# Up projection of an MLP by seven products a pair: the order of the products, a weight difference kept in a tile of its own, and the point from which results are stored

## The chip, the core and the metric

The kernel runs on one core of a Trainium2 chip. The metric is the device time of one execution in microseconds (us); the median of the runs shown is compared. A difference of 0.2% is about 3.1 us here.

## The reference, cut to what matters

The whole layer is computed: a projection, an mLSTM and a forgetting attention side by side, cross attention into 256 memory tokens, then the MLP and a last norm. The change touches the first matrix product of the MLP.

```
u = relu(rmsnorm(x) @ w_ff1)     # x: 1024 tokens x 1024, w_ff1: 1024 x 4096
x = x + (u * u) @ w_ff2          # w_ff2: 4096 x 1024
return rmsnorm(x, ln_f)
```

All of it is float32.

## The kernel before, in words

**Three passes for a product.** TensorE multiplies a rounded type, `fp32r`. A float32 operand is split in a high part (ScalarE, L132) and the rest (VectorE, L133); `mm3` (L182) then makes three matmuls, low times high, high times low and high times high, with lines L184, L185 and L186.

**Seven products for a pair.** The up projection takes the 32 output tiles of 128 in 16 pairs. Of a pair, weights and activations are cut in 2 x 2 blocks (two output tiles, two halves of the 1024 inputs, two halves of the 1024 tokens), and the four result blocks come out of seven block products with sums of blocks, numbered 1 to 7, in place of eight. The right sides (`H`: blocks 11, 21, t1, t2, 22, t3, t4) are made once and lie in SBUF in seven `act` tiles. The left sides are made for each pair by `left_up` (L1185) in three groups: group 0 loads two raw tiles and splits the halves for products 1 and 2 and the half for product 4 (`r_b`, `r_c`), then GpSimd turns the raw tiles into sums and differences in place; group 1 gives products 5 and 6, group 2 gives 7 and 3. One block product is 4 x 3 = 12 matmuls of 128 x 512.

**Three banks for a pair.** Product 1 goes to PSUM bank a, 5 to bank c, 6 to bank b. Product 2 is added into a, 3 into c, 7 and then 4 into b. Between two products of one bank the first has to be read: after 1 ScalarE copies the bank to `p1` (L1339); after 5, 6, 3, 7 and 4 VectorE adds it to a result block (`add`, L1326). So TensorE cannot start 2, 3, 7 or 4 before that read is done. Each finished block is squared after a relu on ScalarE (L1315, L1316).

**The order.** `jobs` lists the products in order. For pairs 2 to 13 it is 1, 4 of the pair before, 5, 2, 6, 3, 7 (L1216); the first two pairs are interleaved product by product, and so are the last two (L1217). `prepare` (L1227) calls a group's left side five jobs ahead. At each job one function of `later` is called: `put_right` (L1369) gives a pair seven such functions after its product 4, which make the right sides of the down projection from the four blocks and store them to DRAM (`put`, L1362: split, then two stores; the high part goes through `r_d` and `r_e` in turn, two tiles each). At every eighth job `stretch` (L1422) loads a 128 x 1024 piece of the residual (`x2d`, L1427), and four jobs later VectorE multiplies it by a row (L1430) and it is stored.

**Who sets the rest.** A scheduler of the framework places each instruction on its engine's queue when the program is built. The engines then run their queues strictly in order, and every DMA is issued by SyncE (SP) in order too. The tiles are shared through pools: three `wh` and three `wl` tiles for a left side's two parts, two tiles each for `r_b`, `r_c`, `r_p`, `r_d`, `r_e`, five `w4`, and eight PSUM banks.

**After it.** The down projection (L1505) loads the stored right sides in the `act` tiles that the up projection frees (`rights`, L1463), and x2d as well (`x2_load`, L1484).

Of the kernel before, what the change touches and what calls it, by code (L numbers as in the profile page):

```python
# [44 lines left out]
def hybrid_layer(ctx: ExitStack, tc: tile.TileContext, a: dict, out: bass.AP):  # L45
# [1139 lines left out]
    def left_up(p_, group):  # L1185
# [5 lines left out]
        hi, lo = (sb(t, [P, 1024], 3, F32R) for t in ("wh", "wl"))  # L1191
        split(hi, lo, (r1, r2, r1)[group])
        if group == 0:
            h22, l22 = (w2(t, dt=F32R) for t in ("bc" if p_ else "ay"))
            split(h22, l22, x22)
            cuts[p_, 4] = both((h22, l22), lambda t: t.rearrange("p (k c) -> p k c", k=4))

            by = g if p_ > 1 else v
            by.tensor_tensor(out=x21, in0=x21, in1=x22, op=ALU.add)
            sub(x22, x21, x11, by)  # L1200
            sub(x12, x12, x22, by)
            sub(x11, h22.bitcast(F32), x22, by)
            by.tensor_tensor(out=x11, in0=x11, in1=l22.bitcast(F32), op=ALU.add)
        for e in range(2):
            cuts[p_, ((1, 2), (5, 6), (7, 3))[group][e]] = both((hi, lo), lambda t: t[:, e * TH : e * TH + TH].rearrange("p (k c) -> p k c", k=4))
        if group == 2:
            del raws[p_]

    raws = {}
    RIGHTS = {1: "11", 2: "21", 5: "t1", 6: "t2", 3: "22", 7: "t3", 4: "t4"}  # L1210
    NP = len(todo)
    both_of = lambda p_: [(q_, i) for i in RIGHTS for q_ in (p_, p_ + 1)]
    jobs = both_of(0)
    for p_ in range(2, NP - 2):

        jobs += [(p_, 1)] + ([(p_ - 1, 4)] if p_ > 2 else []) + [(p_, i) for i in (5, 2, 6, 3, 7)]  # L1216
    jobs += [(NP - 2, 1), (NP - 3, 4)] + both_of(NP - 2)[1:]  # L1217
    GROUP = {1: 0, 2: 0, 5: 1, 6: 1, 7: 2, 3: 2}
# [94 lines left out]
    def squared(x, y):  # L1313

        s.activation(x, y, AF.Relu)  # L1315
        s.activation(x, x, AF.Square)  # L1316

    class Pair:


        def __init__(self, p_):
            self.p_ = p_
            self.u = {}

# [3 lines left out]
        def run(self, i, l):  # L1328
# [8 lines left out]
            if i == 1:  # L1337
                self.p1 = w2("p") if 1 < self.p_ < NP - 2 else row[:, TH * (self.p_ % 2) :][:, :TH]
                s.activation(self.p1, ps, AF.Copy)  # L1339
# [3 lines left out]
            elif i == 5:  # L1343
                t = w4()
                u["22"], self.t1 = t[:, :TH], t[:, TH:]
                self.add(u["22"], ps, self.p1)
# [15 lines left out]
    def put(dst, x):  # L1362

        hi = rotate("d", "e").bitcast(F32R)
        split(hi, x.bitcast(F32R), x)
        load(dst[0], hi.bitcast(F32))
        load(dst[1], x)

    def put_right(b, k, pair):  # L1369

        u11, u12, u21, u22 = (pair.u[c] for c in ("11", "12", "21", "22"))
        t1 = pair.t1
        to = lambda c: [right[b][ORDER.index(c), :, p_, k] for p_ in range(2)]
        t = {}

# [11 lines left out]
        def four():  # L1387
            sub(t[4], t[2], u21)
            put(to("22"), u22)

        return [one, two, lambda: put(to("t3"), u12), four, lambda: put(to("21"), u21), lambda: put(to("t2"), t[2]), lambda: put(to("t4"), t[4])]

# [42 lines left out]
    for at, (p_, i) in enumerate(jobs):  # L1435
# [6 lines left out]
        if at == 30:  # L1442
            to_row(row, inv, 8, rowd[3:4], bank)
        if at > 30 and at % 4 == 0 and stretches:
            stretch(stretches[0])
            if at % 8 == 4:
                stretches.pop(0)
        if at == len(jobs) - 3:
            lefts = left(a["w_ff2q"][0, 0])
        if later:  # L1450
            later.pop(0)()
        pair = pairs.setdefault(p_, Pair(p_))
        pair.run(i, cuts.pop((p_, i)))
        if i == 4:
            b, k = todo[p_][:2]
            later += put_right(b, k, pair) if b < NB - 1 else put_plain(k, pair)
            del pairs[p_]
# [186 lines left out]
```

## Time and profile before

| | us |
|---|---|
| median of 3 runs (1546.37 to 1550.0) | 1548.31 |
| the profiled execution's own time | 1549.03 |
| its span, first to last instruction | 1547.3 |
| TensorE (PE) busy | 1510.3 |
| VectorE (DVE) busy | 1100.9 |
| ScalarE (ACT) busy | 718.8 |
| GpSimd (POOL) busy | 483.4 |

The up projection runs from about 886 to 1216 us of the span. In the profile PE is the matmul engine. A row of the timeline gives the start, the time it took, the engine, the line, what is written and read, and in square brackets how long the engine had been idle before it and what ended that. In a row of a group, the number after the bar is the busy time, then the mean in ns, then the idle time before these instructions and its releasers. A matmul's end is modelled, and matmuls overlap, so the distance from start to start is what one costs.

### The profile page before, as it was taken

The page shows a single profiled execution, that of the slowest core. Times are in us where ns is not written, and L with a number is a line of the kernel's source. Part 1 is how long each engine was busy: PE and PEld are TensorE (multiplying, and loading weights), DVE is VectorE, ACT ScalarE, POOL GpSimd, SP SyncE. Part 2 cuts the span into 40 slices and gives each one's busy share as a digit, 9 for nine tenths or more (in the row PEclk, how much of TensorE's full clock was granted, in tenths as well). Part 3 has the DMA queues.
Part 4 walks back from the last instruction along what each step waited for, and adds up shares of the span by engine and source line. Part 5 has one row for each costly group of instructions (what it writes and reads, how often), then busy time and mean ns, then how long its engine had stood idle before and what let it go on. Part 6 is the DMA issues. An engine that isn't in the chain of part 4 may idle for free.

```text
span 1547.3 us, 21934 instructions
## 1 busy us (share of the span) xinstructions
PE 1510.3 (98%) x7729; PEld 1261.5 (82%) x7729; DVE 1100.9 (71%) x1722; ACT 718.8 (46%) x1337; POOL 483.4 (31%) x515
## 2 busy tenths in 40 slices
PE   8999999999999999999999999999999999999997
PEld 8878888889898887788888788777778778888887
DVE  7656676665788874854457987777777787777766
ACT  7324343334678763543344456555455532222234
POOL 0002130413455441511110034453444644433310
PEclk9999999999999999999999999999999999999998
DMA  6422223436887948953344446776776965556623
GB/s 220 122 79 82 100 100 114 130 130 162 253 248 219 305 166 286 327 176 124 122 147 153 150 148 230 268 253 230 250 243 219 370 251 217 219 207 227 236 92 110
DMA packets 118075, 297.25 MB, mean 192 GB/s; under 512 B 13118, under 2 KB 27768, under 8 KB 111820
## 3 DMA queue, kind: packets, MB, share of 16 engines
q1 hardware_dynamic: 117964, 295.84, 55.9%
q8 instruction: 61, 1.00, 0.3%
q14 instruction: 50, 0.41, 0.1%
HBM read 199.08 MB, written 96.71 MB: 191 GB/s over the span
## 4 chain that ended last, share of the span: by engine, by line
PE 82%; DMA 7%; DVE 6%; issue 2%; ACT 2%; POOL 0%; SPq 0%; DVEq 0%; POOLq 0%; ACTq 0%
PE tp L184 7%; PE tp L186 7%; PE tp L185 7%; PE mm L184 5%; PE sc L184 5%; PE sc L186 5%; PE sc L185 5%; PE mm L186 5%; PE mm L185 5%; PE m L184 5%; PE m L186 5%; PE m L185 5%; PE ov L184 2%; PE ov L185 2%; PE ov L186 2%
## 5 line engine op out<-in xcount | busy, mean ns | idle before, releaser
L184 PE MATMUL tp<-act,wl 128*128 128x512 f32 (+1 forms) x448 | 176.1, 394 | 4.8 <-DVE r_f L1326 3.4
L185 PE MATMUL tp<-act,wh 128*128 128x512 f32 (+1 forms) x448 | 175.3, 391 | 0.0
L186 PE MATMUL tp<-act,wh 128*128 128x512 f32 (+1 forms) x448 | 174.9, 392 | 0.0
L133 DVE TENSOR_TENSOR wl<-wr,wh 128x1024 fp32r<-128x1024 f32 (+2 forms) x99 | 126.3, 1276 | 26.7 <-ACT wh L132 26.3
L132 ACT ACTIVATE wh<-wr 128x1024 fp32r<-128x1024 f32 (+2 forms) x99 | 99.0, 1000 | 94.5 <-PE tp L186 32.7
L184 PE MATMUL mm<-act,wl 128*128 128x512 f32 (+1 forms) x336 | 130.6, 389 | 3.5 <-DVE r_e L1071 1.3
L186 PE MATMUL mm<-act,wh 128*128 128x512 f32 (+1 forms) x336 | 129.0, 384 | 0.0
L185 PE MATMUL mm<-act,wh 128*128 128x512 f32 (+1 forms) x336 | 128.8, 383 | 0.0
L184 PE MATMUL m<-act,wl 128*128 128x512 f32 (+1 forms) x312 | 120.3, 386 | 0.9 <-DVE r_a L916 0.9
L186 PE MATMUL m<-act,wh 128*128 128x512 f32 (+1 forms) x312 | 119.3, 382 | 0.0
L185 PE MATMUL m<-act,wh 128*128 128x512 f32 (+1 forms) x312 | 119.1, 382 | 0.0
L184 PEld LDWEIGHTS tp<-act,wl 128*128 128x128 f32 x448 | 84.2, 188 | 25.4 <-DVE r_f L1326 3.8
L184 PE MATMUL sc<-act,wl 128*128 128x512 f32 (+1 forms) x252 | 98.7, 392 | 3.8 <-DVE r_f L1326 2.3
L1410 POOL TENSOR_TENSOR z<-wr 128x256 f32<-128x256 f32 x56 | 53.5, 976 | 150.4 <-DMA wr<-w_ff2q 127.9
L186 PEld LDWEIGHTS tp<-act,wh 128*128 128x128 f32 x448 | 84.2, 188 | 19.2
L185 PEld LDWEIGHTS tp<-act,wh 128*128 128x128 f32 x448 | 84.2, 188 | 18.8
L185 PE MATMUL sc<-act,wh 128*128 128x512 f32 (+1 forms) x252 | 98.4, 390 | 0.0
L186 PE MATMUL sc<-act,wh 128*128 128x512 f32 (+1 forms) x252 | 98.3, 391 | 0.0
L132 ACT ACTIVATE w<-wr 128x768 fp32r<-128x768 f32 (+2 forms) x31 | 25.5, 824 | 127.3 <-PE tp L186 70.3
L132 ACT ACTIVATE wh<-z 128x1024 fp32r<-128x1024 f32 (+1 forms) x54 | 55.5, 1027 | 61.1 <-POOL z L1410 27.3
L133 DVE TENSOR_TENSOR wl<-z,wh 128x1024 fp32r<-128x1024 f32 (+1 forms) x54 | 73.1, 1353 | 12.4 <-ACT wh L132 12.3
L184 PEld LDWEIGHTS mm<-act,wl 128*128 128x128 f32 x336 | 63.3, 188 | 17.2 <-DVE wl L133 2.1
(676 smaller groups left out, 4236.8 us busy)
## 6 DMA issues: line engine op xcount, KB each, us to landing
act<-right SPq DMA_DIRECT2D x35, 1024.0 KB
right<-w SPq DMA_DIRECT2D x56, 256.0 KB
wr<-w_ff2q SPq DMA_DIRECT2D x28, 512.0 KB
act<-fqk SPq DMA_DIRECT2D x48, 256.0 KB
wr<-w_in SPq DMA_DIRECT2D x20, 512.0 KB
wr<-w_ff SPq DMA_DIRECT2D x20, 512.0 KB
right<-r_e SPq DMA_DIRECT2D x35, 256.0 KB
right<-r_d SPq DMA_DIRECT2D x35, 256.0 KB
```

The source lines that it names most:

```text
L132: s.activation(hi, src, AF.Copy)
L133: return v.tensor_tensor(out=lo, in0=src, in1=hi.bitcast(F32), op=ALU.subtract)
L184: nc.tensor.matmul(ps, w[1], x[0], start=first, stop=False, skip_group_check=more)
L185: nc.tensor.matmul(ps, w[0], x[1], start=False, stop=False, skip_group_check=more)
L186: nc.tensor.matmul(ps, w[0], x[0], start=False, stop=last, skip_group_check=more)
L1410: g.tensor_tensor(out=o, in0=x, in1=y, op=op)
```

## The change

- **Order of the products.** For pairs 2 to 14 it is now 1, 5, 6, 2, 4 of the pair before, 3, 7. The last pair has an order of its own: 1, 6, 4 of pair 14, 5, 7, 2, 3, 4. The first two pairs keep theirs. Of two products into one bank (1 and 2, 5 and 3, 6 and 7, 7 and 4) at least two others stand between from pair 2 on; before, one stood between 6 and 7 and one between 7 and 4.
- **A tile for a difference.** The difference x11 - x21, which product 7 needs, was computed back from the split parts of x22 into the raw tile by two GpSimd instructions at the end of a group's chain. It is now the first instruction of the chain and goes to an `r_e` tile (`thirds`). The chain has four instructions and not five; group 2 splits its two halves apart (two instructions of 512 columns and not one of 1024, on ScalarE and on VectorE). `put` now uses `r_d` alone.
- **Stores.** `put_right` is called twice: four functions after product 7 and three after product 4. Of `later`, two are called at a job when more than five wait.
- **x2d pieces.** `stretch` loads at jobs divisible by 8 and multiplies seven jobs later, and not four.
- The tiles of the last pairs change: `p1` takes `r_p` there too, and the last pair's block 22 takes the half of a `w4` tile that pair 14 doesn't use.

```diff
@@ -1189,32 +1189,36 @@
         r1, r2 = raws[p_]
         x11, x12, x21, x22 = r1[:, :TH], r1[:, TH:], r2[:, :TH], r2[:, TH:]
         hi, lo = (sb(t, [P, 1024], 3, F32R) for t in ("wh", "wl"))
-        split(hi, lo, (r1, r2, r1)[group])
+        if group < 2:
+            split(hi, lo, (r1, r2)[group])
+        else:
+            for c, x in ((slice(0, TH), x12), (slice(TH, 2 * TH), thirds.pop(p_))):
+                split(hi[:, c], lo[:, c], x)
         if group == 0:
             h22, l22 = (w2(t, dt=F32R) for t in ("bc" if p_ else "ay"))
             split(h22, l22, x22)
             cuts[p_, 4] = both((h22, l22), lambda t: t.rearrange("p (k c) -> p k c", k=4))
 
             by = g if p_ > 1 else v
+            s3 = thirds[p_] = w2("e") if p_ > 1 else x11
+            sub(s3, x11, x21, by)
             by.tensor_tensor(out=x21, in0=x21, in1=x22, op=ALU.add)
-            sub(x22, x21, x11, by)
+            sub(x22, x22, s3, by)
             sub(x12, x12, x22, by)
-            sub(x11, h22.bitcast(F32), x22, by)
-            by.tensor_tensor(out=x11, in0=x11, in1=l22.bitcast(F32), op=ALU.add)
         for e in range(2):
-            cuts[p_, ((1, 2), (5, 6), (7, 3))[group][e]] = both((hi, lo), lambda t: t[:, e * TH : e * TH + TH].rearrange("p (k c) -> p k c", k=4))
+            cuts[p_, ((1, 2), (5, 6), (3, 7))[group][e]] = both((hi, lo), lambda t: t[:, e * TH : e * TH + TH].rearrange("p (k c) -> p k c", k=4))
         if group == 2:
             del raws[p_]
 
-    raws = {}
+    raws, thirds = {}, {}
     RIGHTS = {1: "11", 2: "21", 5: "t1", 6: "t2", 3: "22", 7: "t3", 4: "t4"}
     NP = len(todo)
     both_of = lambda p_: [(q_, i) for i in RIGHTS for q_ in (p_, p_ + 1)]
     jobs = both_of(0)
-    for p_ in range(2, NP - 2):
-
-        jobs += [(p_, 1)] + ([(p_ - 1, 4)] if p_ > 2 else []) + [(p_, i) for i in (5, 2, 6, 3, 7)]
-    jobs += [(NP - 2, 1), (NP - 3, 4)] + both_of(NP - 2)[1:]
+    for p_ in range(2, NP - 1):
+
+        jobs += [(p_, i) for i in (1, 5, 6, 2)] + ([(p_ - 1, 4)] if p_ > 2 else []) + [(p_, 3), (p_, 7)]
+    jobs += [(NP - 1, 1), (NP - 1, 6), (NP - 2, 4)] + [(NP - 1, i) for i in (5, 7, 2, 3, 4)]
     GROUP = {1: 0, 2: 0, 5: 1, 6: 1, 7: 2, 3: 2}
     first = {}
     for at, (p_, i) in enumerate(jobs):
...
@@ -1361,17 +1372,16 @@
 
     def put(dst, x):
 
-        hi = rotate("d", "e").bitcast(F32R)
+        hi = w2("d", dt=F32R)
         split(hi, x.bitcast(F32R), x)
         load(dst[0], hi.bitcast(F32))
         load(dst[1], x)
 
-    def put_right(b, k, pair):
-
-        u11, u12, u21, u22 = (pair.u[c] for c in ("11", "12", "21", "22"))
-        t1 = pair.t1
+    def put_right(b, k, pair, last):
+
+        u, t1, t = pair.u, pair.t1, pair.t
+        u11, u12, u22 = (u[c] for c in ("11", "12", "22"))
         to = lambda c: [right[b][ORDER.index(c), :, p_, k] for p_ in range(2)]
-        t = {}
 
         def one():
             sub(t1, u12, u11)
@@ -1385,10 +1395,12 @@
             load(to("t1")[1], t1)
 
         def four():
-            sub(t[4], t[2], u21)
-            put(to("22"), u22)
-
-        return [one, two, lambda: put(to("t3"), u12), four, lambda: put(to("21"), u21), lambda: put(to("t2"), t[2]), lambda: put(to("t4"), t[4])]
+            sub(t[4], t[2], u["21"])
+            put(to("21"), u["21"])
+
+        if last:
+            return [four, lambda: put(to("t2"), t[2]), lambda: put(to("t4"), t[4])]
+        return [one, two, lambda: put(to("t3"), u12), lambda: put(to("22"), u22)]
 
     def put_plain(k, pair):
         f = lambda i, hf: lambda: put([plain[2 * i + k, :, p_, hf] for p_ in range(2)], pair.u[f"{i + 1}{hf + 1}"])
@@ -1441,19 +1453,23 @@
             norm_factors(1)
         if at == 30:
             to_row(row, inv, 8, rowd[3:4], bank)
-        if at > 30 and at % 4 == 0 and stretches:
+        if at > 31 and at % 8 in (0, 7) and stretches:
             stretch(stretches[0])
-            if at % 8 == 4:
+            if at % 8 == 7:
                 stretches.pop(0)
         if at == len(jobs) - 3:
             lefts = left(a["w_ff2q"][0, 0])
-        if later:
-            later.pop(0)()
+        for _ in range(2 if len(later) > 5 else 1):
+            if later:
+                later.pop(0)()
         pair = pairs.setdefault(p_, Pair(p_))
         pair.run(i, cuts.pop((p_, i)))
+        b, k = todo[p_][:2]
+        if i in (7, 4) and b < NB - 1:
+            later += put_right(b, k, pair, i == 4)
+        elif i == 4:
+            later += put_plain(k, pair)
         if i == 4:
-            b, k = todo[p_][:2]
-            later += put_right(b, k, pair) if b < NB - 1 else put_plain(k, pair)
             del pairs[p_]
     for f in later:
         f()
```

Left out of the diff are the new tiles of the last pairs (the last bullet). The rows below are each engine's queue as the program has it, in order: line, operation, tile written, tiles read, partitions by columns. The numbers in a name tell one tile from another.

VectorE before, around the addition of product 4 of a pair, after the x2d piece's multiplication (L1430): `sc_1884` holds product 4 and `sc_1908` product 6 of the next pair, `r_b_1898` and `r_c_1899` are the two parts of the half that the left side of the pair after that needs for its own product 4, and `wl_1897` is its group 0.

```order
L1430 TENSOR_TENSOR w4_1923_10699<-w4_1923_10699,row_79 128x1024
L1326 TENSOR_TENSOR r_p_1868_10331<-sc_1884_10421,r_p_1868_10331 128x512
L133 TENSOR_TENSOR r_c_1899_10527<-wr_1895_10519,r_b_1898_10526 128x512
L1166 TENSOR_TENSOR w4_1916_10663<-w4_1916_10663,r_p_1868_10331 128x512
L133 TENSOR_TENSOR r_p_1868_10331<-r_p_1868_10331,r_e_1931_10746 128x512
L133 TENSOR_TENSOR w4_1916_10663<-w4_1916_10663,r_d_1934_10766 128x512
L1326 TENSOR_TENSOR r_f_1909_10598<-sc_1908_10585,r_p_1891_10495 128x512
L133 TENSOR_TENSOR wl_1897_10523<-wr_1894_10518,wh_1896_10522 128x1024
L133 TENSOR_TENSOR w4_1916_10663<-w4_1916_10663,r_e_1935_10788 128x512
L1326 TENSOR_TENSOR r_f_1909_10598<-tp_1901_10540,r_f_1909_10598 128x512
```

The addition of product 6 to `r_f_1909` stands seventh, behind the piece, the addition of 4, the `r_c` split, a difference and two splits of `put`. The same place after the change, where `r_p_1855` gets product 4 from `sc_1866`, `r_f_1892` gets product 6 from `sc_1891` and then 3 from `tp_1881`, and `wl_1886` and `wl_1894` are groups 0 and 1 of one left side:

```order
L1332 TENSOR_TENSOR r_f_1892_10428<-sc_1891_10415,r_p_1880_10375 128x512
L133 TENSOR_TENSOR wl_1886_10399<-z4_1883_10394,wh_1885_10398 128x1024
L1442 TENSOR_TENSOR w4_1905_10543<-w4_1905_10543,row_79 128x1024
L1332 TENSOR_TENSOR r_p_1855_10207<-sc_1866_10247,r_p_1855_10207 128x512
L133 TENSOR_TENSOR r_c_1888_10403<-z4_1884_10395,r_b_1887_10402 128x512
L1166 TENSOR_TENSOR w4_1890_10411<-w4_1890_10411,r_p_1855_10207 128x512
L1332 TENSOR_TENSOR r_f_1892_10428<-tp_1881_10379,r_f_1892_10428 128x512
L133 TENSOR_TENSOR r_p_1855_10207<-r_p_1855_10207,r_d_1898_10475 128x512
L133 TENSOR_TENSOR w4_1890_10411<-w4_1890_10411,r_d_1899_10495 128x512
L133 TENSOR_TENSOR wl_1894_10431<-z4_1884_10395,wh_1893_10430 128x1024
```

The addition of 6 now stands first, ahead of the piece, and the addition of 4 behind it. Behind 4 stand the same splits and the addition of 3, and group 1's `wl` ends the list.

GpSimd before, the chain of a left side (`wr_1894` and `wr_1895` are the raw tiles; a row writes one half of a tile), with the sum x21 + x22 of the next left side ahead of it and a difference of a finished pair's blocks behind it:

```order
L1199 TENSOR_TENSOR z4_1918_10683<-z4_1918_10683 128x512
L1166 TENSOR_TENSOR wr_1895_10519<-wr_1895_10519,wr_1894_10518 128x512
L1166 TENSOR_TENSOR wr_1894_10518<-wr_1894_10518,wr_1895_10519 128x512
L1166 TENSOR_TENSOR wr_1894_10518<-r_b_1898_10526,wr_1895_10519 128x512
L1203 TENSOR_TENSOR wr_1894_10518<-wr_1894_10518,r_c_1899_10527 128x512
L1166 TENSOR_TENSOR r_f_1909_10598<-w4_1902_10553,r_f_1909_10598 128x512
```

And after, where `z4_1883` and `z4_1884` are the raw tiles of such a chain, the first two rows and `wr_1908` and `wr_1909` being of the next left side:

```order
L1166 TENSOR_TENSOR r_e_1914_10574<-wr_1908_10562,wr_1909_10563 128x512
L1205 TENSOR_TENSOR wr_1909_10563<-wr_1909_10563 128x512
L1166 TENSOR_TENSOR z4_1884_10395<-z4_1884_10395,r_e_1889_10406 128x512
L1166 TENSOR_TENSOR z4_1883_10394<-z4_1883_10394,z4_1884_10395 128x512
L1166 TENSOR_TENSOR r_f_1892_10428<-w4_1882_10392,r_f_1892_10428 128x512
```

The instructions that read `r_b` and `r_c` are gone, and one that writes an `r_e` tile stands first.

SyncE before, from a piece's load (L1427) to its store (L1431):

```order
L1427 DMA w4_1923_10699<-x2d_7240 128x1024
L1366 DMA right3_7244<-r_d_1927_10722 128x512
L1366 DMA right3_7244<-r_e_1924_10701 128x512
L1367 DMA right3_7244<-w4_1878_10387 128x512
L1367 DMA right3_7244<-r_f_1885_10434 128x512
L1366 DMA right3_7244<-r_d_1934_10766 128x512
L1431 DMA x2d_7240<-w4_1923_10699 128x1024
```

And after:

```order
L1439 DMA w4_1905_10543<-x2d_7240 128x1024
L1378 DMA right3_7244<-r_f_1867_10260 128x512
L1377 DMA right3_7244<-r_d_1897_10454 128x512
L1378 DMA right3_7244<-w4_1857_10224 128x512
L1443 DMA x2d_7240<-w4_1905_10543 128x1024
```

Between load and store stand three stores of `put` and not five, though three more jobs lie between them.

More of the change, by code (lines that the diff above doesn't have):

```diff
@@ L1316, in squared @@
         s.activation(x, x, AF.Square)
+    unused = []
     class Pair:
@@ L1322, in __init__ @@
             self.p_ = p_
-            self.u = {}
+            self.u, self.t = {}, {}
         def add(self, out_, ps, x):
@@ L1337, in run @@
             if i == 1:
-                self.p1 = w2("p") if 1 < self.p_ < NP - 2 else row[:, TH * (self.p_ % 2) :][:, :TH]
+                self.p1 = w2("p") if self.p_ > 1 else row[:, TH * (self.p_ % 2) :][:, :TH]
                 s.activation(self.p1, ps, AF.Copy)
@@ L1343, in run @@
             elif i == 5:
-                t = w4()
-                u["22"], self.t1 = t[:, :TH], t[:, TH:]
+                if self.p_ == NP - 1:
+                    u["22"] = unused.pop()
+                else:
+                    t = w4()
+                    u["22"], self.t1 = t[:, :TH], t[:, TH:]
+                    if self.p_ == NP - 2:
+                        unused.append(self.t1)
                 self.add(u["22"], ps, self.p1)
```

## Prediction, on record before the run

> **What bounds the kernel now.** I began with the page's line of busy times:
>
> ```profile
> PE 1510.3 (98%) x7729; PEld 1261.5 (82%) x7729; DVE 1100.9 (71%) x1722; ACT 718.8 (46%) x1337; POOL 483.4 (31%) x515
> ```
>
> TensorE is busy for 98%, so a change that removes none of its matmuls can gain only where it waits. Next I read the windows of the up projection and of the passage to the down projection. The columns are the stretch, its length, the busy time of PE, PEld, DVE, ACT and POOL, the granted clock, the DMA share and GB/s:
>
> ```profile
> 906.00:1206.00 300.00, 289.70 (x1231) 231.42 (x1230) 229.67 (x254) 169.15 (x261) 143.65 (x93) 0.99 0.69 238
> 1206.00:1260.00 54.00, 53.60 (x229) 42.51 (x228) 45.41 (x59) 23.11 (x31) 30.22 (x30) 1.00 1.00 379
> ```
>
> PE idles 10.3 us of 300 in the first stretch and 0.4 of 54 in the second, where the DMA engines are full. 16 pairs of 7 products of 12 matmuls are 1344 matmuls, as many after as before. The timeline of PE has the waits of the stage one by one (start, time, what ran, and the idle before it):
>
> ```profile
> 889.51 0.50 PE L184 MATMUL tp<-act,wl 128*128 128x512 f32 x1 [0.74 <-ACT row L1339]
> 1000.65 0.50 PE L184 MATMUL tp<-act,wl 128*128 128x512 f32 x1 [3.37 <-DVE r_f L1326]
> 1021.50 0.50 PE L184 MATMUL mm<-act,wl 128*128 128x512 f32 x1 [0.99 <-DVE wl L133]
> 1063.30 0.50 PE L184 MATMUL sc<-act,wl 128*128 128x512 f32 x1 [2.34 <-DVE r_f L1326]
> 1063.64 0.52 PE L185 MATMUL sc<-act,wh 128*128 128x512 f32 x1
> ...
> 1067.29 0.39 PE L185 MATMUL sc<-act,wh 128*128 128x512 f32 x1
> 1067.51 0.39 PE L186 MATMUL sc<-act,wh 128*128 128x512 f32 x1
> ...
> 1126.25 0.50 PE L184 MATMUL ov<-act,wl 128*128 128x512 f32 x1 [2.18 <-DVE r_f L1326]
> 1147.52 0.50 PE L184 MATMUL sc<-act,wl 128*128 128x512 f32 x1 [1.42 <-DVE wl L133]
> 1210.07 0.50 PE L184 MATMUL tp<-act,r_c 128*128 128x512 f32 x1 [0.19 <-DVE w L1326]
> 1239.49 0.50 PE L184 MATMUL mm<-act,wl 128*128 128x512 f32 x1 [0.21 <-DVE wl L133]
> ```
>
> Three large waits end on `r_f` of L1326: product 7 waits for the addition of 6 out of the bank that 7 needs. Two end on `wl`, a left side's low part. A matmul is some 0.39 us long but the next starts 0.22 to 0.235 us after it (1067.29 to 1067.51), so a product of 12 lasts 2.8 us and a pair 19.6, and an idle of x costs x + 0.16. To see why VectorE was late I took its own timeline ahead of the wait at 1063.30, and the issue of the piece's load:
>
> ```profile
> 1051.46 0.42 SPq L1427 DMA_DIRECT2D w<-x2d  x1
> ```
>
> ```profile
> 1056.90 1.23 DVE L1430 TENSOR_TENSOR w<-w,row 128x1024 f32<-128x1024 f32 x1 [2.22 <-DMA w<-x2d]
> 1058.04 0.68 DVE L1326 TENSOR_TENSOR r_p<-sc,r_p 128x512 f32<-128x512 f32 x1
> 1058.64 0.69 DVE L133 TENSOR_TENSOR r_c<-wr,r_b 128x512 fp32r<-128x512 f32 x1
> 1060.09 1.16 DVE L1166 TENSOR_TENSOR w<-w,r_p 128x512 f32<-128x512 f32 x1 [0.76 <-ACT r_p L1316]
> 1061.35 0.69 DVE L133 TENSOR_TENSOR r_p<-r_p,r_e 128x512 fp32r<-128x512 f32 x1
> 1061.96 0.69 DVE L133 TENSOR_TENSOR w<-w,r_d 128x512 fp32r<-128x512 f32 x1
> 1062.56 0.68 DVE L1326 TENSOR_TENSOR r_f<-sc,r_p 128x512 f32<-128x512 f32 x1
> 1063.16 1.22 DVE L133 TENSOR_TENSOR wl<-wr,wh 128x1024 fp32r<-128x1024 f32 x1
> ```
>
> The piece landed 5.4 us after its issue, VectorE stood 2.22 us for it, and six instructions later the addition of 6 ended at 1063.24, just before PE went on. The group of that line sums it up:
>
> ```profile
> L1430 DVE TENSOR_TENSOR w<-w,row 128x1024 f32<-128x1024 f32 x8 | 10.2, 1275 | 19.0 <-DMA w<-x2d 19.0
> ```
>
> All eight pieces were waited for, 2.4 us on the average. Only one product (2.8 us) lies between 6 and 7, so what VectorE loses there reaches PE.
>
> **The waits that go.** After the change 3 or more products stand between 6 and 7 as the pairs run (2, 4, 3), that is 8.4 us and not 2.8, and the addition of 6 stands ahead of the piece in VectorE's queue. The longest wait, 3.37 us, is less than the 5.6 us gained, so I count the three waits for `r_f` gone: 3.37 + 2.34 + 2.18 = 7.89. The two on `wl` (0.99 + 1.42 = 2.41) come from the same delay: `wl` is the instruction behind the addition of 6 in the list above. SyncE's queue also moves: the piece's load is issued behind a store of `put` that follows product 1 of the pair, some 1.8 us after that product (two ACT steps of about 0.64, as the splits below, and the issue's 0.42); the multiplication cannot come before group 0's `wl`, which waits for the end of product 2, 8.4 us behind product 1. That gives the load 9 us for its 5.4, so the 19.0 us of VectorE go too. What is late next is group 1's `wl`, below.
>
> Five waits: 10.30 idle, and 5 x 0.16 = 0.8 for the pipeline. The first step after a wait is 0.34 and not 0.235 (1063.30 to 1063.64): 5 x 0.1 = 0.5. And from 1063.64 to 1067.29 PE took 3.65 us for ten steps that are 2.34 else: 1.3 at half clock, following the wait. Sum 12.9. The Trainium skill ("TensorE: Matmul & The Clock Gate", What's actually happening) has the clock fall after an idle window of about 3.4 us that runs free of the program. This trace shows the fall behind an idle of 2.34 and none behind 3.37, so it doesn't bear out a threshold on the wait alone; if the 1.3 us hung on something else than this wait, they would stay, and the forecast below would be 1.3 us higher.
>
> The waits of 0.74 (first pairs, order kept) and 0.19 and 0.21 (last pairs) I leave as they are; if the last two went too, 0.4 + 2 x 0.16 = 0.7 more would be gained.
>
> **The new chain.** Product 4 of a pair now stands fifth in the next pair, and frees `r_b` and `r_c`, two tiles each. Call its end E. From there: ACT splits `r_b`, DVE `r_c`, GpSimd subtracts in the raw tile, ACT makes group 1's `wh`, DVE its `wl`, and product 5 of the pair after needs it at E + 8.4 (3, 7 and 1 lie between). Before, seven products did, 19.6 us. The rows at such an end, and the groups of the steps in 906 to 1206:
>
> ```profile
> 1011.72 0.39 PE L186 MATMUL ov<-act,wh 128*128 128x512 f32 x1
> ```
>
> ```profile
> 1011.92 0.64 ACT L132 ACTIVATE r_b<-wr 128x512 fp32r<-128x512 f32 x1 [1.84 <-PE tp L186]
> 1011.92 0.69 DVE L1326 TENSOR_TENSOR r_p<-tp,r_p 128x512 f32<-128x512 f32 x1 [1.11 <-PE tp L186]
> ```
>
> ```profile
> L133 DVE TENSOR_TENSOR wl<-wr,wh 128x1024 fp32r<-128x1024 f32 x22 | 33.2, 1513 | 5.1 <-ACT wh L132 5.1
> L1166 DVE TENSOR_TENSOR w<-w,r_p 128x512 f32<-128x512 f32 x12 | 15.1, 1260 | 2.6 <-ACT r_p L1316 2.5
> L133 DVE TENSOR_TENSOR r_c<-z,r_b 128x512 fp32r<-128x512 f32 x7 | 7.0, 998 | 0.3 <-ACT r_b L132 0.3
> L133 DVE TENSOR_TENSOR w<-w,r_d 128x512 fp32r<-128x512 f32 x21 | 17.5, 835 | 1.6 <-ACT r_d L132 1.1
> L133 DVE TENSOR_TENSOR r_p<-r_p,r_e 128x512 fp32r<-128x512 f32 x6 | 6.3, 1049 | 0.1
> ```
>
> ```profile
> L132 ACT ACTIVATE wh<-wr 128x1024 fp32r<-128x1024 f32 x22 | 23.2, 1053 | 10.1 <-POOL wr L1203 5.1 <-POOL wr L1166 2.3 <-PE sc L186 1.7
> L1315 ACT ACTIVATE r_p<-r_p 128x512 f32<-128x512 f32 x12 | 7.6, 630 | 11.3 <-DVE r_p L1326 11.1
> ```
>
> ```profile
> L1166 POOL TENSOR_TENSOR z<-z,z 128x512 f32<-128x512 f32 x14 | 21.1, 1505 | 30.2 <-DVE wl L133 17.7 <-DVE r_c L133 11.8 <-POOL z L1199 0.7
> L1166 POOL TENSOR_TENSOR z<-r_b,z 128x512 f32<-128x512 f32 x7 | 14.0, 1994 | 0.0
> L1203 POOL TENSOR_TENSOR z<-z,r_c 128x512 f32<-128x512 f32 x7 | 11.9, 1702 | 0.5
> ```
>
> VectorE's queue behind E holds, with the means, the addition of 4 (0.2 after E, 0.7), `r_c` (0.85, between 0.69 and 1.0), the wait for the relu and the square (2 x 0.63 behind the addition), the difference (1.26), the addition of 3 (0.7), two low parts of `put` (0.85 and 1.05) and `wl` (1.5): it ends at E + 7.5, 0.9 us early. In the eight pairs with a piece, group 0's `wl` starts at E - 1.75 (the end of product 2 and an ACT split of 1.05 behind it), ends at E - 0.2, and the piece's 1.28 puts the addition of 4 at E + 1.25 and `wl`'s end, the same row of steps on, at E + 8.5 to 8.8. That is 0.1 to 0.4 us late; I take 0.25, the middle, in eight pairs: **+2.0**. The bounds are 0 (at the quickest rows of the timeline, 0.69 and 1.22, it is on time) and 0.4 + 0.16 in each of the 12 pairs, 6.7.
>
> **What costs nothing.** GpSimd loses the 1.99 and the 1.70 us of two instructions per pair and gains one of 1.5. Group 2's two splits of 512 are 2 x 0.63 on ACT for 1.05, and 2 x 0.69 on DVE for 1.22: 0.2 more on each. They are hidden by engines that are idle for 131 us (ACT) and 70 us (DVE) of the 300; without cover they would cost 0.2 in each of 13 pairs, 2.6, which the chain's upper bound holds.
>
> **The passage to the down projection.** There the DMA engines are full (1.00, 379 GB/s), and the last pair's own order frees the `act` tiles later; a tile of 128 x 2048 float32 is 1 MB, 2.8 us at that rate. If one comes late, PE waits for up to that; if `r_d`'s stores block the queue as well, 4. Before, PE lost 0.4 in 54 us there. Bounds 0 and 4; I take **+0.5**, nearest to what the window shows.
>
> **The sum.** 1549.03 - 12.9 + 2.0 + 0.5 = 1538.6 for an execution like the profiled one, which lies 0.7 above the median of the runs: 1537.9.
>
> **The rivals.** *Half of the gain is given back:* the chain late in all 12 pairs by 0.4 + 0.16, 6.7 and not 2.0: 1537.9 + 4.7 = 1542.6 (the passage at its bound gives 1541.4). For it: the waits of ACT's `wh` for GpSimd (5.1 and 2.3 above) show that this hand-off is already the slow one. Against it: two GpSimd steps are gone from it. *The waits only move:* VectorE's additions are late for another reason than the piece, and others take their place: about 1548. Against it: all three waits for `r_f` lie behind a wait for a piece.
>
> *Slower:* `put` uses two `r_d` tiles and not four tiles, so ACT's split waits for the store of two puts ago; the VectorE split of `put` waits with it, and behind it in the queue stands group 1's `wl`, for which PE waits in every pair. It decides from the point where `wl` ends later than E + 8.4; at E + 9.6 it is 1.24 + 0.16 = 1.4 in 12 pairs, 17 us: 1549.03 - 12.9 + 17 + 0.5 - 0.7 = 1553. It makes up for the whole gain from 1.1 us a pair. For it: the piece's load took 5.4 us to land, and two puts are 5.6 us apart at one a job. Against it: VectorE waited only 1.1 us in 21 splits for `r_d`. The Trainium skill ("GPSIMD Engine Reference", Key points) says that GpSimd shares its SBUF interfaces with VectorE and contends with its instructions of two SBUF inputs; the trace agrees, with `wl` at 1.22 alone and 1.51 in the mean. It would lengthen this chain, and the means used here hold it already.
>
> **How the numbers follow.** 0.2%, 3.1 us, is about what a measurement of this kernel can tell from no change. The forecast has 0.70 (its own range 1534 to 1541), half the gain given back 0.14, no change 0.08, slower 0.08. Faster is the first two: 0.84. The range begins at 1533.5: no late chain, no cost in the passage and the 0.7 of the last pairs gone give 1537.9 - 3.2 = 1534.7, and runs scatter by 1 to 2 us. It ends at 1545.5, where the chain costs 6.7 and the passage 3.4, and leaves out the last two cases.
>
> **What the profile after would show.** Right: no wait for a piece on DVE's L1442, no wait of PE for `r_f`, PE's idle in the stage at about 3 us and not 11.4 (10.30 + 0.74 + 0.19 + 0.21), small waits for group 1's `wl` in pairs with a piece. Wrong: waits of PE for `wl` in most pairs, 0.4 us or more each; ACT waiting for stores ahead of `r_d`; PE waiting for `act` loads behind the last pair; or the same waits for additions at other products.

## The result and the profile after

The changed kernel takes 1535.09 us (median of 4 runs, 1534.38 to 1535.7), the kernel before 1547.58 beside it. The ratio is 0.9911, with a 95% interval of 0.9899 to 0.9924: faster by 12.5 us. The forecast was 1537.9 us, faster, in a range of 1533.5 to 1545.5.

The page's line of busy times, and the windows of the up projection and of the passage behind it:

```profile
PE 1507.4 (98%) x7729; PEld 1263.2 (82%) x7729; DVE 1104.6 (72%) x1736; ACT 721.8 (47%) x1353; POOL 456.4 (30%) x501
```

```profile
906.00:1206.00 300.00, 300.00 (x1288) 241.89 (x1287) 241.96 (x282) 183.25 (x293) 127.21 (x89) 1.00 0.71 254
1206.00:1260.00 54.00, 54.00 (x234) 43.53 (x233) 45.06 (x60) 16.16 (x19) 24.64 (x24) 1.00 0.82 310
```

PE has no idle left in either stretch, where it had 10.3 and 0.4 us, and its clock is 1.00 and not 0.99. The whole list of PE's waits from 886 to 1262 us is one row, the wait in the first pairs, which the change leaves alone (what waited, for whom, us in total, times, longest):

```profile
PE tp L184 <- ACT row L1345: 0.7, 1, 0.7
```

It stands 0.44 us earlier than before, and that is all that the work ahead of the stage adds:

```profile
889.07 0.50 PE L184 MATMUL tp<-act,wl 128*128 128x512 f32 x1 [0.73 <-ACT row L1345]
```

The spans are 1547.3 and 1532.6, 14.7 apart. So 14.2 us come from the stage and the passage: the 10.7 of idle, a restart of about 0.26 behind each of the seven waits, and the half clock behind one. The profiled execution of before is 1.45 us above the median of its runs and that of after 0.7 below, which is why their difference is larger than the 12.5.

### The profile page after: what moved, and what is told of

It is laid out like the page before. It is cut to its first block, busy times and chain, and to the rows that moved or that the text cites. A ratio compares the mean times of both kernels' runs of the same rounds, so it can differ in the third digit from the quotient of the medians.

```text
span 1532.6 us, 21930 instructions
## 1 busy us (share of the span) xinstructions
PE 1507.4 (98%) x7729; PEld 1263.2 (82%) x7729; DVE 1104.6 (72%) x1736; ACT 721.8 (47%) x1353; POOL 456.4 (30%) x501
## 4 chain that ended last, share of the span: by engine, by line
PE 92%; DMA 3%; DVE 2%; ACT 1%; issue 1%; POOL 0%; SPq 0%; DVEq 0%; POOLq 0%; ACTq 0%
PE tp L184 8%; PE tp L186 8%; PE tp L185 8%; PE sc L184 6%; PE sc L186 6%; PE sc L185 6%; PE mm L184 6%; PE mm L186 6%; PE mm L185 6%; PE m L184 6%; PE m L186 6%; PE m L185 6%; PE ov L779 2%; PE ov L184 2%; PE ov L185 2%; PE ov L186 2%
## 5 line engine op out<-in xcount | busy, mean ns | idle before, releaser
L184 PE MATMUL tp<-act,wl 128*128 128x512 f32 (+1 forms) x440 | 172.5, 393 | 0.7 <-ACT row L1345 0.7
L185 PE MATMUL tp<-act,wh 128*128 128x512 f32 (+1 forms) x440 | 172.2, 391 | 0.0
L186 PE MATMUL tp<-act,wh 128*128 128x512 f32 (+1 forms) x440 | 172.0, 392 | 0.0
L132 ACT ACTIVATE wh<-wr 128x1024 fp32r<-128x1024 f32 (+3 forms) x100 | 96.1, 962 | 104.0 <-PE tp L186 39.7
L133 DVE TENSOR_TENSOR wl<-wr,wh 128x1024 fp32r<-128x1024 f32 (+3 forms) x100 | 120.2, 1203 | 21.7 <-ACT wh L132 21.3
L186 PE MATMUL mm<-act,wh 128*128 128x512 f32 (+1 forms) x344 | 132.2, 384 | 0.0
L185 PE MATMUL mm<-act,wh 128*128 128x512 f32 (+1 forms) x344 | 132.0, 384 | 0.0
L132 ACT ACTIVATE wh<-z 128x1024 fp32r<-128x1024 f32 (+2 forms) x55 | 52.5, 956 | 66.0 <-POOL z L1422 29.4
L133 DVE TENSOR_TENSOR wl<-z,wh 128x1024 fp32r<-128x1024 f32 (+2 forms) x55 | 67.0, 1219 | 12.0 <-ACT wh L132 11.9
```

Source lines behind the costliest of these rows:

```text
L132: s.activation(hi, src, AF.Copy)
L133: return v.tensor_tensor(out=lo, in0=src, in1=hi.bitcast(F32), op=ALU.subtract)
L184: nc.tensor.matmul(ps, w[1], x[0], start=first, stop=False, skip_group_check=more)
L185: nc.tensor.matmul(ps, w[0], x[1], start=False, stop=False, skip_group_check=more)
L186: nc.tensor.matmul(ps, w[0], x[0], start=False, stop=last, skip_group_check=more)
```

## The experiments

All are compared with the kernel before on the same chip, whose median lay between 1547 and 1551 us from chip to chip, so the ratios are what compares. "The two GpSimd instructions" are the last two of the old chain of a left side, which compute x11 - x21 from `r_b` and `r_c` for product 7.

| kernel | order | pieces | the two GpSimd instructions | ratio to before (95%) | PE idle, 906 to 1206 |
|---|---|---|---|---|---|
| before | old | yes | yes | 1 | 10.3 |
| no piece | old | none | yes | 0.9924 (0.9902 to 0.9946) | 1.7 |
| old order, rest changed | old | yes | gone | 0.9993 (0.998 to 1.0005) | 9.9 |
| order alone | new | yes | yes | 1.0035 (1.002 to 1.005) | 15.7 |
| order alone, no piece | new | none | yes | 0.9962 (0.9943 to 0.998) | 6.3 |
| order less two | new | yes | left out | 0.9887 (0.9873 to 0.9902) | 0 |
| changed | new | yes | gone | 0.9911 (0.9899 to 0.9924) | 0 |
| changed, two put back as dead work | new | yes | dead | 1.004 (1.0024 to 1.0056) | 15.3 |

### The order alone, and the order without it

The new order for pairs 2 to 13 in the kernel before:

```diff
-        jobs += [(p_, 1)] + ([(p_ - 1, 4)] if p_ > 2 else []) + [(p_, i) for i in (5, 2, 6, 3, 7)]
+        jobs += [(p_, i) for i in (1, 5, 6, 2)] + ([(p_ - 1, 4)] if p_ > 2 else []) + [(p_, 3), (p_, 7)]
```

> The kernel before with the new order of the products for pairs 2 to 13 alone; the last two pairs, the left sides' chain, the stores and the four jobs between a piece's load and its multiplication are as before. If the distance between the products of one bank is what gains (14.2 us of PE's steps between 900 and 1260 us went in the changed kernel's profile), nearly all of the gain is here: 1535 to 1537 us, no wait of PE for r_f, at most the two small waits of the last pairs (0.7 together). If the weight difference's own tile, the stores or the seven jobs carry a part, it lies at 1538 to 1545 and PE waits for VectorE in the profile. If the shorter chain needs the new tile (five GpSimd instructions behind E and not four, the r_b and r_c held longer), PE waits for wl in most pairs: 1545 or more.

It took 1554.29 us, ratio 1.0035 (1.002 to 1.005): slower than before. PE's waits:

```profile
PE m L184 <- DVE wl L133: 6.1, 2, 4.1
PE sc L184 <- DVE wl L133: 4.1, 4, 2.3
PE tp L184 <- DVE wl L133: 3.6, 2, 2.2
PE mm L184 <- DVE wl L133: 1.2, 1, 1.2
PE tp L184 <- ACT row L1339: 0.7, 1, 0.7
PE ov L184 <- DVE wl L133: 0.6, 1, 0.6
```

No wait for `r_f` is left, as the spacing between 6 and 7 should do. In their place stand ten waits for group 1's `wl`, 15.6 us. That product spacing alone gains fell here; the third theory, that the order needs the new chain, fits.

The other way round, the changed kernel with the old list of jobs, last pairs included:

```diff
-    for p_ in range(2, NP - 1):
-        jobs += [(p_, i) for i in (1, 5, 6, 2)] + ([(p_ - 1, 4)] if p_ > 2 else []) + [(p_, 3), (p_, 7)]
-    jobs += [(NP - 1, 1), (NP - 1, 6), (NP - 2, 4)] + [(NP - 1, i) for i in (5, 7, 2, 3, 4)]
+    for p_ in range(2, NP - 2):
+        jobs += [(p_, 1)] + ([(p_ - 1, 4)] if p_ > 2 else []) + [(p_, i) for i in (5, 2, 6, 3, 7)]
+    jobs += [(NP - 2, 1), (NP - 3, 4)] + both_of(NP - 2)[1:]
```

> The changed kernel with the old order of the products, all the rest as changed. If the distance between products gains, the waits for the additions of 6 are back: 3 to 5 waits of PE of 1 to 3.4 us, 1545 to 1549. If the other parts of the change gain, it stays at 1535 to 1540.

It took 1548.73 us, ratio 0.9993 (0.998 to 1.0005), no change from before. The waits for additions are there again, 1.6 us in three, and four for `wl` with 8.2. Three of these four come five rows behind a piece ahead of which VectorE had stood for 2.3 to 3.4 us; the longest, 4.0, is in the last pairs and has no piece ahead of it. So neither half gains by itself; the gain is in the two together.

### Four jobs and not seven, and the pieces

```diff
-        if at > 31 and at % 8 in (0, 7) and stretches:
+        if at > 30 and at % 4 == 0 and stretches:
             stretch(stretches[0])
-            if at % 8 == 7:
+            if at % 8 == 4:
```

> The changed kernel with the multiplication of a piece called four jobs after its load, as before, and not seven. The scheduler places both at the same rows of the queues as with seven, all five queues are the same row by row. If so it costs nothing: 1535.1, within 1 us. If the seven jobs do matter (by the tiles' addresses or the waits), VectorE's waits for pieces come back (19 us against 2.2 in the changed kernel), which puts group 1's wl late in 8 pairs: 1538 to 1545.

1534.01 us, ratio 0.9899 (0.9883 to 0.9916): the same as the changed kernel within the intervals. The number of jobs between load and multiplication moves no time, and in the profiles from 886 to 1262 us no instruction: the rows of PE, VectorE, ScalarE and GpSimd stand in the same order in both. The scheduler places both by itself.

The kernel before without the pieces:

```diff
-    stretches = list(range(KT))
+    stretches = []
```

> The kernel before without the eight x2d pieces: their loads, multiplications and stores in the up projection are left out (the residual isn't scaled), the order of the products is the old one. If VectorE's waits for the pieces (19.0 us) are what makes the additions of 6 late, the five waits of PE go here as well: 1534 to 1537. If VectorE is late by its other work and one product between 6 and 7 is too little by itself, waits of PE for r_f stay: 1542 or more.

1536.9 us, ratio 0.9924 (0.9902 to 0.9946). Of PE's five large waits two are left, of 0.8 us:

```profile
PE ov L184 <- DVE r_f L1326: 0.8, 1, 0.8
PE sc L184 <- DVE r_f L1326: 0.8, 1, 0.8
```

In the old order it is the pieces that make the additions late, as the prediction read from the trace. This run leaves out their multiplications (10.2 us) together with the waits for them (19.0 us), so it doesn't tell the two apart.

### The two GpSimd instructions

Put back in the changed kernel behind its chain, where nothing reads what they write:

```diff
-            sub(x12, x12, x22, by)
+            sub(x12, x12, x22, by), p_ > 1 and (sub(x11, h22.bitcast(F32), x22, by), by.tensor_tensor(out=x11, in0=x11, in1=l22.bitcast(F32), op=ALU.add))
```

> The changed kernel with the two GpSimd instructions of the old chain put back behind it as dead work (what they write is not read again). All other queues are row for row those of the changed kernel. In the changed kernel's profile group 1's wl ends 6.7 us behind E in a pair with a piece and is needed at 8.4. In the run with the new order alone the same splits took 1.78 and 2.28 us beside GpSimd and not 0.69 and 1.20. If VectorE is slowed by GpSimd's work beside it, 2.2 us are added there and wl comes 0.5 us late, 0.7 with the restart, in 8 to 12 pairs: 1540 to 1544, and PE waits for wl. If the two instructions only cost where product 7 waits for what they write, nothing changes: 1535, no wait of PE for wl.

1556.59 us, ratio 1.004 (1.0024 to 1.0056): 0.0129 above the changed kernel's ratio, about 20 us for dead work on an engine that is idle most of the time. VectorE behind E (the end of product 4, as in the prediction) in one pair, with GpSimd beside it:

```profile
1044.25 0.68 DVE L1332 TENSOR_TENSOR r_p<-sc,r_p 128x512 f32<-128x512 f32 x1
...
1047.39 0.68 DVE L1332 TENSOR_TENSOR r_f<-tp,r_f 128x512 f32<-128x512 f32 x1
1047.99 1.19 DVE L133 TENSOR_TENSOR r_p<-r_p,r_d 128x512 fp32r<-128x512 f32 x1
1049.11 1.79 DVE L133 TENSOR_TENSOR w<-w,r_d 128x512 fp32r<-128x512 f32 x1
1050.82 2.31 DVE L133 TENSOR_TENSOR wl<-z,wh 128x1024 fp32r<-128x1024 f32 x1
1053.06 0.68 DVE L1332 TENSOR_TENSOR w<-sc,w 128x512 f32<-128x512 f32 x1
```

```profile
1045.61 1.31 POOL L1166 TENSOR_TENSOR z<-z,r_e 128x512 f32<-128x512 f32 x1 [2.36 <-DVE r_c L133]
1047.00 1.64 POOL L1166 TENSOR_TENSOR z<-z,z 128x512 f32<-128x512 f32 x1
1048.59 1.76 POOL L1166 TENSOR_TENSOR z<-r_b,z 128x512 f32<-128x512 f32 x1
1050.42 1.62 POOL L1207 TENSOR_TENSOR z<-z,r_c 128x512 f32<-128x512 f32 x1
```

Now the same steps in the changed kernel, from the addition of 6 to `wl`, and GpSimd:

```profile
1027.55 0.69 DVE L1332 TENSOR_TENSOR r_f<-sc,r_p 128x512 f32<-128x512 f32 x1 [0.17 <-PE sc L186]
1028.65 1.99 DVE L133 TENSOR_TENSOR wl<-z,wh 128x1024 fp32r<-128x1024 f32 x1 [0.40 <-ACT wh L132]
1030.81 2.07 DVE L1442 TENSOR_TENSOR w<-w,row 128x1024 f32<-128x1024 f32 x1 [0.17 <-DMA w<-x2d]
1033.15 0.69 DVE L1332 TENSOR_TENSOR r_p<-sc,r_p 128x512 f32<-128x512 f32 x1 [0.28 <-PE sc L186]
1033.82 0.69 DVE L133 TENSOR_TENSOR r_c<-z,r_b 128x512 fp32r<-128x512 f32 x1
1035.21 1.23 DVE L1166 TENSOR_TENSOR w<-w,r_p 128x512 f32<-128x512 f32 x1 [0.70 <-ACT r_p L1320]
1036.36 0.68 DVE L1332 TENSOR_TENSOR r_f<-tp,r_f 128x512 f32<-128x512 f32 x1
1036.96 1.19 DVE L133 TENSOR_TENSOR r_p<-r_p,r_d 128x512 fp32r<-128x512 f32 x1
1038.07 0.68 DVE L133 TENSOR_TENSOR w<-w,r_d 128x512 fp32r<-128x512 f32 x1
1038.68 1.21 DVE L133 TENSOR_TENSOR wl<-z,wh 128x1024 fp32r<-128x1024 f32 x1
```

```profile
1028.26 1.30 POOL L1166 TENSOR_TENSOR r_e<-wr,wr 128x512 f32<-128x512 f32 x1 [4.26 <-DVE r_f L1332]
1029.64 2.16 POOL L1205 TENSOR_TENSOR wr<-wr 128x512 f32<-128x512 f32 x1
1034.59 1.29 POOL L1166 TENSOR_TENSOR z<-z,r_e 128x512 f32<-128x512 f32 x1 [2.80 <-DVE r_c L133]
1035.97 1.63 POOL L1166 TENSOR_TENSOR z<-z,z 128x512 f32<-128x512 f32 x1
```

Row by row they are alike until GpSimd's two extra rows begin: the split of `w` is then 1.79 and not 0.68, and `wl` 2.31 and not 1.21, 1.1 us more for each, without an idle of VectorE between them. `wl` ends 6.7 us behind the start of the addition of 4 in the changed kernel and 8.9 with the dead work. The addition starts 0.2 us behind E, so that is E + 6.9 and E + 9.1, and PE needs `wl` at E + 8.4 (1041.36, where E is 1032.96). In the pair shown with the dead work the addition is late by 0.65 us more, behind a piece, and PE waits 1.22 us.

The mechanism is VectorE held up by GpSimd, and the rows say how: not by a slower run but by a wait for GpSimd's row to end. The split of `w` ends at 1050.90, 0.55 us behind the GpSimd row that was running when it began (1048.59 to 1050.35), and the split of `r_p` 0.54 behind its own (1049.18 and 1048.64); `wl` ends 1.09 behind (1053.13 and 1052.04). The same rows of the changed kernel give 0.55 (`r_p`, 1038.15 and 1037.60) and 1.08 (the `wl` at 1028.65 and the piece at 1030.81). How much longer a row takes is how much of GpSimd's row was left when it began, less 0.13 us.

How much PE then loses was forecast too low, at 5 to 9 us: the waits are 0.6 to 2.3 us long and not 0.5, in all 12 pairs, the pieces come late as well (VectorE waits 9.9 us for them and not 2.2), and two waits are followed by half clock.

One of the two alone:

```diff
-            sub(x12, x12, x22, by)
+            sub(x12, x12, x22, by), p_ > 1 and sub(x11, h22.bitcast(F32), x22, by)
```

> The changed kernel with one of the two dead GpSimd instructions behind the chain. All other queues are row for row those of the changed kernel. If the deadline at E + 8.4 decides, one slowed split (1.1 us) still fits: wl ends at about E + 7.8, 1535 to 1537 and no wait of PE for wl but perhaps one in a pair whose piece lands late. If GpSimd's work costs in proportion, half of the 21 us: 1545 to 1547.

1540.64 us, ratio 0.9931 (0.9916 to 0.9946): 0.0020 above the changed kernel's ratio, about 3 us (5.5 by the medians, from two chips), and not half of the 20. One row is held up, and `wl` ends as forecast, 7.8 us behind the start of the addition of 4 (1057.93 to 1065.76); most pairs are on time:

```profile
1057.93 0.69 DVE L1332 TENSOR_TENSOR r_p<-sc,r_p 128x512 f32<-128x512 f32 x1 [2.89 <-PE sc L186]
...
1062.85 1.78 DVE L133 TENSOR_TENSOR w<-w,r_d 128x512 fp32r<-128x512 f32 x1
1064.55 1.21 DVE L133 TENSOR_TENSOR wl<-wr,wh 128x1024 fp32r<-128x1024 f32 x1
```

What PE loses is mostly one wait of 3.3 us and the half clock behind it, in a pair where VectorE stood for 5.57 us ahead of a piece's multiplication. So the cost is not in proportion to GpSimd's work: there is a deadline, and one instruction stays inside it.

And the other way round, the order alone without the two instructions from pair 2 on:

```diff
-            sub(x11, h22.bitcast(F32), x22, by)
-            by.tensor_tensor(out=x11, in0=x11, in1=l22.bitcast(F32), op=ALU.add)
+            if p_ < 2: sub(x11, h22.bitcast(F32), x22, by)
+            if p_ < 2: by.tensor_tensor(out=x11, in0=x11, in1=l22.bitcast(F32), op=ALU.add)
```

> The kernel before with the new order alone, and without the last two GpSimd instructions of a left side's chain from pair 2 on (product 7 then multiplies with the raw block and not with the difference). If it is those two beside VectorE's splits that made the order alone slow, wl comes 2.2 us earlier behind E: of the ten waits of 0.5 to 4.1 us one or two are left, 1536 to 1540. If the pieces, for which VectorE still waits, are the larger part, most waits stay: 1545 or more.

1533.99 us, ratio 0.9887 (0.9873 to 0.9902), better than was expected. Its window, and what VectorE waited for at the pieces:

```profile
906.00:1206.00 300.00, 300.00 (x1288) 241.64 (x1287) 221.53 (x268) 184.01 (x277) 97.00 (x72) 1.00 0.74 262
```

```profile
DVE w L1430 <- DMA w<-x2d: 19.2, 7, 3.1
DVE w L1430 <- DMA row<-rowd: 2.3, 1, 2.3
```

VectorE still waits 19.2 us for the pieces, as long as in the kernel before (19.0), and PE idles for 0 of the 300 us. The new order covers those waits; taking them away isn't needed. This kernel has neither the new tile, nor the earlier stores, nor `put` with `r_d` alone.

### The rest of the change

The changed kernel with the old chain, group 2 split whole, and `put` with `r_d` and `r_e` in turn:

```diff
-            s3 = thirds[p_] = w2("e") if p_ > 1 else x11
-            sub(s3, x11, x21, by)
             by.tensor_tensor(out=x21, in0=x21, in1=x22, op=ALU.add)
-            sub(x22, x22, s3, by)
+            sub(x22, x21, x11, by)
             sub(x12, x12, x22, by)
+            sub(x11, h22.bitcast(F32), x22, by)
+            by.tensor_tensor(out=x11, in0=x11, in1=l22.bitcast(F32), op=ALU.add)
...
-        hi = w2("d", dt=F32R)
+        hi = rotate("d", "e").bitcast(F32R)
```

> The changed kernel with the old chain of a left side (five GpSimd instructions, the difference from r_b and r_c, group 2 split whole, put with r_d and r_e in turn); order and stores as changed. If the difference's own tile is what the new order lacked, it goes the way of the order alone: PE waits for wl in most pairs, 1545 to 1554. If the earlier stores were what it lacked, it stays at 1535 to 1538.

1556.85 us, ratio 1.0042 (1.0026 to 1.0058). PE waits for `wl` in 12 pairs of this stage, where the order alone had ten waits; the earlier stores don't help.

All seven steps of `put_right` behind product 4, as before:

```diff
-        if i in (7, 4) and b < NB - 1:
-            later += put_right(b, k, pair, i == 4)
+        if i == 4 and b < NB - 1:
+            later += put_right(b, k, pair, False) + put_right(b, k, pair, True)
```

> The changed kernel with all seven steps of put_right called behind product 4, one at a job, as before. If the stores' point matters little, 1535 to 1537 and at most a small wait. If VectorE's splits of put, now nearer to the chain behind E, are what the earlier call took away, wl is late by 1 to 2 us in most pairs: 1545 or more.

1534.99 us, ratio 0.9902 (0.9882 to 0.9923): the point of the stores costs and gains nothing.

The order alone without pieces, which is the first edit of this section with `stretches` empty:

```diff
-    stretches = list(range(KT))
+    stretches = []
```

> The kernel before with the new order alone, and without the eight x2d pieces (loads, multiplications and stores left out; the residual isn't scaled). The order alone had ten waits of PE for group 1's wl, 15.6 us together, and VectorE waited 4.1 us for the piece ahead of the one looked at. If the pieces make the chain late, the waits go: 1535 to 1538. If the chain is late by itself (VectorE slowed beside GpSimd's fifth instruction), most of the ten stay at 0.5 to 2 us: 1543 or more.

1543.29 us, ratio 0.9962 (0.9943 to 0.998). All ten waits for `wl` are there, each of 0.53 to 0.66 us (6.3 together): what is late without any piece is the chain itself, `wl` ending at E + 9.1. The other 9.3 us of the order alone's 15.6 come from the pieces. Each of the two theories has a part of it.

### Two that did not settle what they were made for

Dead GpSimd work ahead of the chain:

```diff
-            sub(u12, u22, u12, g)
+            sub(u12, u22, u12, g), sub(t[2], u22, t1, g), sub(t[2], u22, t1, g)
```

> The changed kernel with two dead GpSimd instructions more in a pair, as many as in the run with the dead chain, but ahead of the chain and not behind it (GpSimd writes t2 - a block's difference that VectorE has just written - twice again; the value stays). GpSimd then has 3 us more work in the stretch between the block differences and E, where VectorE makes group 0's wl and multiplies the piece, which had 2.3 us to spare. If the place beside group 1's wl is what cost 21 us there, this costs little: 1535 to 1539. If any GpSimd work of that amount costs it, 1550 or more.

1553.84 us, ratio 1.0025 (1.0013 to 1.0036), in the range of the second forecast (1550 or more), but not for its reason. VectorE now waits for GpSimd, because a split of `put` writes in place what the dead work reads:

```profile
DVE w L133 <- POOL w L1166: 35.6, 12, 4.9
```

That wait of 3 us in 12 pairs stands in VectorE's queue ahead of the chain, so the run doesn't tell whether GpSimd's work elsewhere is free.

Product 4 one product later:

```diff
-        jobs += [(p_, i) for i in (1, 5, 6, 2)] + ([(p_ - 1, 4)] if p_ > 2 else []) + [(p_, 3), (p_, 7)]
+        jobs += [(p_, i) for i in (1, 5, 6, 2, 3)] + ([(p_ - 1, 4)] if p_ > 2 else []) + [(p_, 7)]
```

> The changed kernel with product 4 of the pair before one product later (1, 5, 6, 2, 3, 4, 7), so that only 7 and 1 stand between E and product 5: group 1's wl is needed at E + 5.6 and not 8.4. In the changed kernel's profile it ends at E + 6.7. If that deadline is what decides, PE waits 1.1 us and 0.16 for the restart in each of 12 pairs: 15 us, about 1550. If the chain can start earlier by other means, 1535 to 1540.

1539.19 us, ratio 0.9924 (0.9908 to 0.9941). The scheduler did not keep this order: PE starts the fours of two pairs at 1072.97 and 1082.12 us, three products apart, and the one ahead of them at 1042.04. PE waits 2.8 us, for additions (`w`, L1332) and never for `wl`. The deadline was not set as meant, and the run says nothing on it.

## Why the prediction was right, and where not

**The waits that go: right in size.** Five waits, their restarts and the half clock were put at 12.9 us, 13.6 with the last pairs' two small ones; 14.2 went. The half clock was put too low in it: from 1063.64 to 1067.29 there are nine steps and not ten, 2.11 us else, so it cost 1.54 us and not 1.3. Read from the trace, the cause in the old order was right too, as far as the run without pieces shows it: the three large waits for `r_f` shrink to two of 0.8.

**That the order removes them by itself: wrong.** The part on the waits counts the gain to the spacing, and the part on what costs nothing books the loss of two GpSimd instructions as hidden. The order alone is 0.35% slower. It removes the waits for additions, and moves the deadline of `wl` from 19.6 to 8.4 us behind E, where the old chain's GpSimd work makes `wl` end at E + 9.1. The two instructions were hidden in the old order and are not in the new one; without them it ends at E + 6.9. This is the step that failed: an instruction off the path was costed by its own engine's idle time, not by what runs beside it. The forecast took no harm from it only because the change drops both instructions anyway, which is luck: for the order alone the same working would have given a gain.

**The pieces' waits: right that they go, not why.** They fell from 19.0 to 2.2 us. The prediction lets them go by the load's place behind product 1 in the new order. The order alone doesn't do it: they are 22.6 us with it, 19.2 less the two instructions, and 21.5 in the changed kernel with the old chain. They are 7.0 us in the changed kernel with the old order and 0.3 with the late stores, both of which have the new chain and `put` with `r_d` alone; which part of these does it is open. The seven jobs move nothing, and 19.2 us of such waits do no harm in the run without the two instructions.

**The new chain, +2.0: wrong by its whole size.** Two sub-steps failed. Group 0's split was said to wait for the end of product 2 (E - 2.8). It starts at the end of product 6, one product earlier:

```profile
1027.12 0.40 PE L186 MATMUL sc<-act,wh 128*128 128x512 f32 x1
1027.36 0.39 PE L184 MATMUL mm<-act,wl 128*128 128x512 f32 x1
```

```profile
1027.55 1.06 ACT L132 ACTIVATE wh<-z 128x1024 fp32r<-128x1024 f32 x1 [2.37 <-PE sc L186]
```

So although the piece's multiplication is slower (2.07 us), the addition of 4 behind it starts at E + 0.2 and not at E + 1.25. And the group means of before (`wl` 1.51, `r_c` 0.85, a low part 0.85 to 1.05) hold rows that GpSimd's instructions held up; with two of these gone most rows of the chain are the quick ones, `wl` 1.21. The load, by the same, has 5.7 us (1025.1 to 1030.81) and not 9, and 2.2 us of waits remain.

**The passage, +0.5: wrong by its size.** PE is busy for 54.00 of 54 us, and the DMA share fell from 1.00 to 0.82. With 2.0, 0.5, the last pairs' 0.7 and the 0.44 ahead of the stage, 1538.6 becomes 1535.0, and 1534.7 with the half clock at 1.54; the profiled execution took 1534.38. All these terms erred the same way, so the number was inside the range by the range's width and not by errors that cancel.

**The rivals.** The deadline named in the slower one, E + 8.4, decides, and its price was of the right size (1553 is 0.35% above the median of before; the three kernels with the new order and the two instructions lie 0.35 to 0.42% above theirs). Its mechanism was not `put`'s two `r_d` tiles, which the changed kernel has without a wait of PE, but GpSimd beside VectorE. The trace of before held the sign: `wl` at 1.22 alone and 1.51 in the mean. The Trainium skill ("GPSIMD Engine Reference", Key points) says that GpSimd shares its SBUF interfaces with VectorE and contends with instructions of two SBUF inputs; these runs agree (0.68 to 1.79 for two SBUF sources, 0.68 unchanged beside GpSimd for an addition from PSUM). The prediction cited it and took the means as its whole effect.

## What to carry to other kernels

Closing up products to give one bank its distance takes distance from another chain; write down each chain's deadline in the new order, not only that of the wait that goes. Cost an instruction that is dropped or added on GpSimd by VectorE's rows that run beside it, since a row of two SBUF tiles there waits for GpSimd's row to end, while GpSimd itself is idle for half of the stage. Try each half of a change alone: here the half that reads as the cause was slower than the kernel before.

## What the runs showed of the hardware

**VectorE beside GpSimd.** A 128x512 subtraction of two SBUF tiles takes 0.68 us alone and 1.79 beside a GpSimd instruction of two SBUF tiles, a 128x1024 one 1.21 and 2.31: 1.1 us for each GpSimd instruction of 1.6 to 1.8. An addition with one source in PSUM stays at 0.68 beside it (1047.39 to 1048.07, in GpSimd's 1047.00 to 1048.64). Over all profiles, 880 to 1262 us, 413 VectorE rows of two SBUF tiles began with 0.3 us or more of a GpSimd row left. 407 of them ended 0.53 to 0.56 us (128x512) or 1.07 to 1.10 us (128x1024) behind that row, however much of it was left. GpSimd waits likewise: a row that began in the `wl` at 1028.65 to 1030.64 ended 1.16 us behind it (1031.80) and took 2.16 us, where the row ahead of it took 1.30. So the two take turns, and the 1.1 us is VectorE's wait for one GpSimd row.

**Half clock behind short waits.** Over all profiles, none of the 25 idles of PE of 0.9 to 1.75 us from 886 to 1262 us was followed by half clock (a granted clock of 0.50, steps of 0.43 us and not 0.235). From 1.79 us on 13 of 16 were, for 6 to 10 matmuls. Twelve of these cost about 1.5 us and one 2.2; the 3 idles without it were 1.89, 2.18 and 3.37 us long. The Trainium skill ("TensorE: Matmul & The Clock Gate", What's actually happening) gives an idle window of about 3.4 us for the fall to half clock; here half of that could do, and 3.37 could not.
